# Deep sub-products of a down projection added from PSUM into running totals, with double weight tiles and a wider spread

## The chip, the cores and the metric

One core of a Trainium2 chip runs the kernel. The metric is the device time of one execution in microseconds; the time before is a median of 3 runs. TensorE (PE) multiplies, VectorE (DVE) and ScalarE (ACT) work element by element, GpSimd (POOL) and SyncE (SP) here mostly start DMAs.

## What is computed

A decoder layer on 512 tokens, model width 2048, fp32: attention in two head groups, then a gated feed-forward part with a causal convolution of width 3, then a final RMSNorm. The change lies in the feed-forward part:

```python
def conv_ffn(h, w_up, conv_w, conv_b, w_down):
    u, g = jnp.split(h @ w_up, 2, axis=-1)
    u = lax.conv_general_dilated(u, conv_w[:, None, :], ..., feature_group_count=D_FF) + conv_b
    return (jax.nn.silu(u) * g) @ w_down
...
    mod = c_act @ w_mod[l] + b_mod[l]
...
    x = x + g2 * conv_ffn(h, w_up[l], conv_w[l], conv_b[l], w_down[l])
return rms_norm(x, norm_final)
```

The hidden width is 5632: 44 tiles of 128 columns, in 11 groups of 4 (g = 0 to 10).

## The kernel before

Every fp32 product is made of three fp32r matmuls: each operand is cut into a high part (a cast on ScalarE) and a low part (a subtraction on VectorE), and high x high, low x high and high x low are summed in PSUM.

**Up slots.** A tile f of the hidden width needs two units, u and g, each of four slots; a slot loads 256 KB of w_up through SP (`raw`, 5 buffers), splits it (4 buffers of each part) and issues 12 matmuls of 128x512. So a group has 32 up slots. After unit g of a tile, `conv_gen` makes the convolution, silu and the gate.

**Down products.** The down projection of group g-1 runs among the up slots of group g. A 2x2 block scheme with seven products is used (L1066 to L1241). Four of them, `PLAIN` = 0, 2, 3, 5, run twice (for two halves of columns, c), as `Product`: 12 matmuls each. The other three, `DEEP` = 1, 4, 6, are cut once more by the same scheme into seven sub-products of 3 matmuls, class `Deep`, in four steps: sub-products (0, 1), (2, 3), (4, 5), (6). `Quads` loads the weight blocks (256 KB tiles `rq`), the `STEPS` and `STEPS2` tables say which blocks are added on VectorE before and after a split, and `cut_w` (L1082) splits a 128x512 block into `dh` and `dl`, 4 buffers each.

**Where sums go.** `total[h][dq]` are eight DRAM tiles of 512 KB. A plain product is combined on VectorE straight from PSUM (`plus`, L1162) and added to totals by accumulating DMAs on POOL's queue (`add_up`, L1116). A deep product isn't: each of its seven results is moved by ScalarE into a pair tile (L1230; the ring `two` has 3 pair tiles) and added by an accumulating DMA to a DRAM tile `part[i, j]` of its own, four DMAs a product. Only after the last group does `join_gen` (L1243) load the parts through SP, make the seven sums of each deep product on VectorE (`JOIN`, L1262), add the totals (L1270), transpose (`cT`, TensorE) and add the result, times its gate, to the residual x (`x2b`, L1280).

**The order of slots.** For groups 1 to 10, three up slots (`LEAD`), then 20 down products and 20 up slots in turn, then the other 9 up slots. In group 10 the mark `join` is set behind the 20 pairs: there the pool `pd` is closed, `pe` opens in its place, x is loaded from DRAM (`x2b`, 4 x 1 MB, SP) and `join_gen` is started, one step a slot. Then come `last_slots`: the last group's down projection in plain form, two halves of the tokens x 4 column blocks x 4 slots of 12 matmuls of 128x256. Its weights (`wd`, 16 x 256 KB, SP) are split into the space of the up operands h2h and h2l. A final norm (`finish_half`) closes each half.

**The modulation stream.** `mod_gen` (L236) makes one group of columns of the modulation from 16 pieces: a 256 KB load through SP and one VectorE multiply-add into `macc` (L207) a piece, then column sums on TensorE (`mps`, two passes of 4 matmuls), then an addition of the bias. `pace(gen, every)` calls it for one step each time TensorE has been given `every` more columns. Four groups (20 to 23) run beside groups 0 and 1, with tiles of `pd`.

A planner (the tile framework) fixes the order on each engine from priorities in program order and from what is ready by its own estimate; at run time every engine runs its queue in that order.

```python
    slots += up[:LEAD]
    products = down_products(g - 1)
    for x, y in zip(products, up[LEAD:]):
        slots += [x, y]
    if g == SG:
        marks["join"] = len(slots)
    slots += up[LEAD + len(products):]
```

Of the kernel before, what the change touches and what calls it, by code (L numbers as in the profile page):

```python
# [33 lines left out]
def hybrid_trunk(ctx, tc, xT, cT, wm, bm, nrm, wik, wiq, wi1, sinks, kvn, wuk, wuv, rel, onehot,  # L34
# [201 lines left out]
    def mod_gen(groups, load, depth, mp, get, per):  # L236
# [4 lines left out]
        for i, (g, kt) in enumerate(pieces):  # L241
# [740 lines left out]
    DH, LEAD = 4, 3  # L982
# [82 lines left out]
    class Quads:  # L1065


        BUFS = {0: 4, 1: 2, 2: 4, 3: 4}
# [4 lines left out]
        def load(self, i, c):  # L1073
            if (i, 0, c) in self.b:
# [21 lines left out]
    STEPS2 = [((), 0, ((0, 1, 0),), 0),  # L1096
              ((), 2, (), 1),
              (((1, 3, 1), (0, 3, "t")), "t", (("t", 2, 2),), 3),
              ((), 1, (), 4),
              ((), 2, (), 2),  # L1100
              ((), 0, (), 6),
              ((), 3, (), 5)]

    SIGN = [1, 1, -1, -1, 1, -1, -1]

    JOIN = ((2, 0), (1, 0), (3, 2), (6, 2), (4, 3), (6, 5), (5, 3))
    RESULT = {(0, 0): 1, (0, 1): 6, (1, 0): 4, (1, 1): 5}
    part = {(i, j): dram.tile([P, 2, T], F32, name=f"part{i}_{j}") for i in DEEP for j in range(4)}

# [6 lines left out]
    def add_up(g, to, x):  # L1116
        if g:
# [4 lines left out]
    class Product:  # L1122
# [9 lines left out]
        def split(self):  # L1132
            if self.w is None:
                self.load()
                _, before, blk, behind = STEPS[self.i]
                b, c, rows = self.quads.b, self.c, range(2)
                for p in rows:
                    for x, y, z in before:
                        dve.tensor_tensor(b[z, p, c], b[x, p, c], b[y, p, c], OP.add)  # L1139
                self.w = [cut_w(b[blk, p, c], f"{self.g}_{self.i}_{c}_{p}") for p in rows]  # L1140
                for p in rows:
                    for x, y, z in behind:
# [418 lines left out]
```

## Time and profile before

| | |
|---|---|
| time, median of 3 runs | 2205.28 us (2203.07 to 2211.99) |
| the profiled execution | 2205.46 us, its span 2203.4 us |
| busy: TensorE, VectorE, ScalarE, GpSimd | 2136.7, 1691.1, 1159.0, 249.2 us |
| chain that ended last, by engine | TensorE 80%, VectorE 7%, DMA 5%, ScalarE 4%, issue 3% |
| DMA | 438.18 MB, mean 199 GB/s |
| mean granted TensorE clock | 0.989 |
| accumulates to part / to total | 120 / 80 DMAs |
| down weights rq | 200 DMAs of 256 KB |

Busy times are shares of one execution with stages of different kinds: attention to about 600 us, its output projection to 774 us, the feed-forward part from there. Matmuls are pipelined and their ends modelled, so a row's duration overlaps the next; the distance between starts is what one costs.

### The profile page before, as it was taken

How to read it: one execution, taken by the hardware profiler on the slowest of the kernel's cores; microseconds unless marked ns; L12 is line 12 of the kernel's file. 1: busy time of each engine (PE TensorE's matmuls, PEld its weight loads, DVE VectorE, ACT ScalarE, POOL GpSimd, SP SyncE). 2: the span in 40 equal slices, each digit the busy share in tenths (PEclk: the TensorE clock that was granted, in tenths of full speed). 3: DMA queues.
4: the chain of work that ended last, by engine and by line, in shares of the span. 5: the costliest groups of instructions: out<-in, count | busy, mean ns of one | idle time of the engine just before them, and what ended most of it. 6: DMA issues, size and time to landing. Idle time of an engine off the chain costs nothing.

```text
span 2203.4 us, 30851 instructions
## 1 busy us (share of the span) xinstructions
PE 2136.7 (97%) x10286; PEld 1734.3 (79%) x10286; DVE 1691.1 (77%) x3193; ACT 1159.0 (53%) x2290; POOL 249.2 (11%) x368
## 2 busy tenths in 40 slices
PE   7999998999999999999999999999999999999976
PEld 4777776777778877888888888888888888888866
DVE  3887899777677678987868686877877686877677
ACT  5334977777622263464646555464645555554622
POOL 0000000111133100010201011110201020110200
PEclk9999999999999999999999999999999999999999
DMA  9782221676598648776949696786949596886982
GB/s 390 267 296 80 63 72 56 205 216 209 184 338 273 223 147 279 253 249 150 241 127 228 162 207 191 172 231 153 247 123 242 152 211 176 183 222 147 211 279 100
DMA packets 180800, 438.18 MB, mean 199 GB/s; under 512 B 20703, under 2 KB 27887, under 8 KB 174496
## 3 DMA queue, kind: packets, MB, share of 16 engines
q1 hardware_dynamic: 136256, 286.80, 38.9%
q0 software_dynamic: 43520, 147.84, 30.8%
q8 instruction: 80, 1.31, 0.2%
q10 hardware_dynamic: 864, 1.57, 0.2%
q14 instruction: 80, 0.66, 0.1%
HBM read 328.92 MB, written 107.22 MB: 198 GB/s over the span
## 4 chain that ended last, share of the span: by engine, by line
PE 80%; DVE 7%; DMA 5%; ACT 4%; issue 3%; POOL 0%; SPq 0%; DVEq 0%; POOLq 0%; ACTq 0%
PE p L53 10%; PE qip L53 4%; DMA mraw<-in_wm_dram 3%; PE ckv L53 1%; PE mrow L53 1%; PE p_3s L53 1%; PE p_2s L53 1%; PE p_6s L53 1%; PE p_5s L53 1%; PE p_4s L53 1%; PE p_1s L53 1%; PE p_0s L53 1%; PE o L53 1%; DVE macc L207 1%; DVE wk L668 1%
## 5 line engine op out<-in xcount | busy, mean ns | idle before, releaser
L207 DVE SCALAR_TENSOR_TENSOR macc<-mraw,cact,macc 128x512 f32<-128x512 f32 x240 | 179.7, 749 | 16.6 <-DMA mraw<-in_wm_dram 13.9
L193 ACT CAST dh<-rq 128x512 fp32r<-128x512 f32 x160 | 99.2, 622 | 103.7 <-DVE rq L1139 54.0
L194 DVE TENSOR_TENSOR dl<-rq,dh 128x512 fp32r<-128x512 f32 x160 | 109.2, 688 | 27.4 <-ACT dh L193 25.9
L53 PE MATMUL p<-dl,ah 128*128 128x512 f32 x320 | 124.5, 389 | 0.0
L53 PE MATMUL p<-dh,ah 128*128 128x512 f32 x320 | 124.5, 389 | 0.0
L53 PE MATMUL p<-dh,al 128*128 128x512 f32 x320 | 124.5, 389 | 0.0
L53 PEld LDWEIGHTS p<-dl,ah 128*128 128x128 f32 x320 | 60.1, 188 | 12.5
L53 PEld LDWEIGHTS p<-dh,ah 128*128 128x128 f32 x320 | 60.1, 188 | 12.5
L53 PEld LDWEIGHTS p<-dh,al 128*128 128x128 f32 x320 | 60.1, 188 | 12.5
L1384 POOL DMA_DIRECT2D mraw<-in_wm_dram x48 | 25.5, 532 | 351.1 <-DVE macc L207 232.1
L1432 POOL DMA_DIRECT2D mraw<-in_wm_dram x96 | 51.6, 538 | 116.7 <-DVE macc L207 83.8
L1118 POOL DMA_DIRECT2D total<-e x18 | 15.3, 852 | 366.8 <-ACT e L1170 366.8
L193 ACT CAST bh<-op 128x256 fp32r<-128x256 f32 (+1 forms) x120 | 42.3, 378 | 24.2 <-DVE op L1059 23.1
L1139 DVE TENSOR_TENSOR rq<-rq,rq 128x512 f32<-128x512 f32 x80 | 53.2, 686 | 1.6 <-DMA rq<-in_wdn_dram 1.3
L1143 DVE TENSOR_TENSOR rq<-rq,rq 128x512 f32<-128x512 f32 x80 | 53.4, 688 | 0.9
L523 DVE TENSOR_TENSOR qi<-qi,qip 128x512 f32<-128x512 f32 x56 | 38.3, 685 | 14.4 <-PE qip L53 13.6
L194 DVE TENSOR_TENSOR bl<-op,bh 128x256 fp32r<-128x256 f32 (+1 forms) x120 | 44.7, 388 | 3.4 <-ACT bh L193 0.6
L785 ACT ACTIVATE sb<-sb,nmb 128x512 f32<-128x512 f32 (+2 forms) x64 | 35.3, 553 | 14.7 <-DVE nmb L783 14.7
L422 DVE SCALAR_TENSOR_TENSOR macc<-mraw,cact,macc 128x512 f32<-128x512 f32 x54 | 40.4, 748 | 0.4
L1118 POOL DMA_DIRECT2D total<-u x18 | 15.3, 850 | 192.4 <-DVE u L1162 192.4
L53 PEld LDWEIGHTS mps<-ones,macc 128*128 128x128 f32 x192 | 25.4, 198 | 13.0 <-issue 9.3
L783 DVE CUSTOM_DVE_ANT_0 sb<-scb,tbb 128x512 f32<-128x512 f32 (+2 forms) x64 | 28.5, 487 | 8.6 <-PE scb L53 8.5
(4578 smaller groups left out, 7291.4 us busy)
## 6 DMA issues: line engine op xcount, KB each, us to landing
rq<-in_wdn_dram SPq DMA_DIRECT2D x200, 256.0 KB
mraw<-in_wm_dram SPq DMA_DIRECT2D x32, 1024.0 KB
mraw<-in_wm_dram POOLq DMA_DIRECT2D x48, 512.0 KB, 6.6
mraw<-in_wm_dram POOLq DMA_DIRECT2D x96, 256.0 KB, 5.3
mraw<-in_wm_dram SPq DMA_DIRECT2D x64, 256.0 KB
part<-e_0s POOLq DMA_DIRECT2D x30, 512.0 KB, 8.0
part<-e_2s POOLq DMA_DIRECT2D x30, 512.0 KB, 8.1
part<-e_4s POOLq DMA_DIRECT2D x30, 512.0 KB, 7.8
```

The costliest lines, as they stand in the source:

```text
L53: return self.to.matmul(out, w, x, **kw)
L193: act.copy(hi_t, full)
L194: dve.tensor_tensor(lo_t, full, hi_t.bitcast(F32), OP.subtract)
L207: tc.keep_in_program_order(dve.scalar_tensor_tensor(acc, t, cact[:, kt:kt + 1], acc, OP.mult, OP.add))
L422: dve.scalar_tensor_tensor(acc, fetched[j, q][:, kt % 4], cact[:, kt:kt + 1], acc, OP.mult, OP.add)
L523: dve.tensor_tensor(qi[i], qi[i], ps, OP.add)
L783: dve.tensor_tensor_reduce(s[:, o:o + n], where[b], bias, 1.0, self.nsk, OP.add, OP.min, accum_out=nm[:, b:b + 1])
L785: act.activation(s[:, o:o + n], s[:, o:o + n], AF.Exp, bias=nm[:, b:b + 1], scale=-1.0, accum_out=den[:, b:b + 1])
L1118: pool.dma_start(to, x, accum_op=OP.add)
L1139: dve.tensor_tensor(b[z, p, c], b[x, p, c], b[y, p, c], OP.add)
L1143: dve.tensor_tensor(b[z, p, c], b[x, p, c], b[y, p, c], OP.add)
L1432: pool.dma_start(t, wm[g, kt // 4][:, kt % 4])
```

## The change

Each deep product is combined on VectorE from PSUM, as the plain ones are: step 0 moves one result by ScalarE, the other six (one of them used twice) are added or subtracted by seven VectorE operations into two pair tiles r0 and r1, which are added to the same totals by two accumulating DMAs (`more=True`: also for group 0). The steps become (0, 1), (2), (3, 6), (5, 4). `part`, `JOIN` and `RESULT` go, and so does the summing in `join_gen`; it loads the totals by POOL into four tiles `ct` and transposes from these.

Weight blocks of two rows are one tile of 128x2x512: half as many loads, block sums, casts and subtractions, each twice as wide; half as many buffers.

The slots are spread wider: two up slots behind each of a deep product's first three steps (in group 10, one behind its second), one behind the others. So the products end with the up slots; in group 10 three up slots remain behind the join, in place of nine.

The modulation stream beside groups 0 and 1 gets one empty step ahead of each column sum (`gap`), and its steps come each 3100 columns in place of 3300.

```diff
-    def mod_gen(groups, load, depth, mp, get, per):
+    def mod_gen(groups, load, depth, mp, get, per, gap=0):
...
             if kt == KT - 1:
+                for _ in range(gap):
+                    yield
                 ps = get(f"mps{g}")
...
-        BUFS = {0: 4, 1: 2, 2: 4, 3: 4}
+        BUFS = {0: 2, 1: 1, 2: 2, 3: 2}
...
-            for p in range(2):
-                t = env["pd"].tile([P, 512], F32, tag=f"rq{tag}", bufs=self.BUFS[tag], name=f"rq{self.g}_{i}_{c}_{p}")
-                sp.dma_start(t, wdn[self.g, c + 2 * (at % 2)][:, 2 * (at // 2) + p])
-                self.b[i, p, c] = t
+            t = env["pd"].tile([P, 2, 512], F32, tag=f"rq{tag}", bufs=self.BUFS[tag], name=f"rq{self.g}_{i}_{c}")
+            sp.dma_start(t, wdn[self.g, c + 2 * (at % 2)][:, 2 * (at // 2):2 * (at // 2) + 2])
+            self.b[i, c] = t
     def cut_w(x, n):
-        hi_t = env["pd"].tile([P, 512], F32R, tag="dh", bufs=DH, name=f"dh{n}")
-        lo_t = env["pd"].tile([P, 512], F32R, tag="dl", bufs=DH, name=f"dl{n}")
-        split_to(hi_t, lo_t, x)
-        return hi_t, lo_t
+        hi_t = env["pd"].tile([P, 2, 512], F32R, tag="dh", bufs=2, name=f"dh{n}")
+        lo_t = env["pd"].tile([P, 2, 512], F32R, tag="dl", bufs=2, name=f"dl{n}")
+        k = x.shape[1]
+        split_to(hi_t[:, :k], lo_t[:, :k], x)
+        return [(hi_t[:, i], lo_t[:, i]) for i in range(k)]
...
+    STEPS2 = [((0, 1), (), 0, ((0, 1, 0),)),
+              ((2,), ((1, 3, 1), (0, 3, "t")), "t", (("t", 2, 2),)),
+              ((3, 6), (), 1, ()),
+              ((5, 4), (), 0, ())]
+    OPERAND = [0, 1, 3, 4, 2, 6, 5]
...
-    def add_up(g, to, x):
-        if g:
+    def add_up(g, to, x, more=False):
+        if g or more:
             pool.dma_start(to, x, accum_op=OP.add)
...
         def out(self):
-            g, i, j0, n = self.g, self.i, self.subs[0], len(self.subs)
-            t = pair_tile(f"e{g}_{i}_{j0}s")
-            for k, (j, ps) in enumerate(zip(self.subs, self.ps)):
-                act.mul(t[:, k], ps, float(SIGN[i] * SIGN[j]))
-            add_up(g, part[i, j0 // 2][:, :n], t[:, :n])
+
+            i, box = self.i, self.box
+            n = f"{self.g}_{i}s"
+            h, dq = {1: (0, 0), 4: (1, 0), 6: (0, 2)}[i]
+
+            def plus(to, x, j):
+                dve.tensor_tensor(to, x, self.ps[j], OP.add if SIGN[i] * SIGN[j] > 0 else OP.subtract)
+
+            if self.step == 0:
+                box["r1"] = pair_tile(f"r1{n}")
+                act.mul(box["r1"][:, 0], self.ps[0], float(SIGN[i] * SIGN[0]))
+                box["r0"] = pair_tile(f"r0{n}")
+                plus(box["r0"][:, 0], box["r1"][:, 0], 1)
+                return
+            r0, r1 = box["r0"], box["r1"]
+            if self.step == 1:
+                plus(r1[:, 0], r1[:, 0], 2)
+            elif self.step == 2:
+                plus(r0[:, 1], r1[:, 0], 3)
+                plus(r1[:, 0], r1[:, 0], 6)
+            else:
+                plus(r1[:, 1], r0[:, 1], 5)
+                plus(r1[:, 0], r1[:, 0], 5)
+                add_up(self.g, total[h][dq + 1], r1, True)
+                plus(r0[:, 1], r0[:, 1], 4)
+                add_up(self.g, total[h][dq], r0, True)
...
-        yield from deep(1, 0, 0)
-        yield from deep(4, 1, 0)
...
+        for dq in range(4):
+            ct = []
+            for h in range(2):
+                t = env["pe"].tile([P, 2, T], F32, tag="ct", bufs=4, name=f"ct{dq}_{h}")
+                pool.dma_start(t, total[h][dq])
+                ct += [t[:, 0], t[:, 1]]
             for i in range(4):
                 ps = p_ps(f"cT{dq}_{i}", (P, 4, P))
                 for tb in range(NB):
-                    pe.transpose(ps[:, tb], ready[tb, dq][:, P * i:P * i + P], ident)
+                    pe.transpose(ps[:, tb], ct[tb][:, P * i:P * i + P], ident)
...
-        products = down_products(g - 1)
-        for x, y in zip(products, up[LEAD:]):
-            slots += [x, y]
+        at = LEAD
+        for i, x in enumerate(down_products(g - 1)):
+            n = 1 if i < 8 or i % 4 == 3 else 2
+            if g == SG and i % 4 == 1:
+                n = 1
+            slots += [x] + up[at:at + n]
+            at += n
         if g == SG:
             marks["join"] = len(slots)
-        slots += up[LEAD + len(products):]
+        slots += up[at:]
...
-    pace(mod_gen(range(20, 24), pd_mod, 4, p2, o_bank, 1), 3300)
+    pace(mod_gen(range(20, 24), pd_mod, 4, p2, o_bank, 1, 1), 3100)
```

## Rows read from the trace of the kernel before

**Rows 1.** The page, busy time, share of the span and instructions.

```profile
PE 2136.7 (97%) x10286; PEld 1734.3 (79%) x10286; DVE 1691.1 (77%) x3193; ACT 1159.0 (53%) x2290; POOL 249.2 (11%) x368
```

**Rows 2.** The chain in order of time: start us, us, what.

```profile
1003.36 8.16 PE u8ps L53 x36
...
1988.00 8.16 PE u40ps L53 x36
```

**Rows 3.** TensorE's timeline in group 0: start us, us, engine, line, operation.

```profile
865.67 1.75 PE L53 MATMUL mps<-ones,macc 128*128 128x1 f32 x8 [4.17 <-DVE macc L207]
867.29 0.77 PE L53 MATMUL g3ps<-h2h,g3r_1h 128*128 128x512 f32 x1
...
873.04 0.40 PE L53 MATMUL g3ps<-h2h,g3r_2l 128*128 128x512 f32 x1
```

**Rows 4.** The chain's last stretch.

```profile
2159.51 1.10 PE d_1ps L53 x7
...
2187.11 1.45 PE d_3ps L53 x12
```

**Rows 5.** TensorE's timeline, transposes of the join.

```profile
2127.16 1.31 PE L57 MATMUL cT<-identr,res 128*128 128x128 f32 x8 [0.41 <-DVE x2b L1280]
```

**Rows 6.** Windows at the end: stretch us, busy by engine, granted clock, DMA, GB/s.

```profile
2090.00:2100.00 10.00, 10.00 (x45) 8.28 (x45) 2.72 (x5) 1.87 (x3) 0.00 (x0) 1.00 1.02 394
2105.00:2110.00 5.00, 1.75 (x7) 0.77 (x5) 4.34 (x8) 1.24 (x2) 0.00 (x0) 0.82 0.62 187
2110.00:2115.00 5.00, 4.49 (x12) 3.11 (x11) 3.78 (x7) 0.62 (x1) 0.00 (x0) 0.50 1.00 336
2105.00:2160.00 55.00, 40.07 (x247) 32.39 (x246) 46.76 (x82) 14.07 (x27) 0.00 (x0) 0.94 0.65 216
2140.00:2145.00 5.00, 2.75 (x21) 2.34 (x20) 5.00 (x9) 1.21 (x2) 0.00 (x0) 1.00 0.57 163
```

**Rows 7.** Waits from 2083.7 to 2170: total us, times, longest us.

```profile
ACT h2h L193 <- DMA wd<-in_wdn_dram: 23.5, 9, 3.8
...
SPq L1249 <- DVE sub L1262: 6.2, 2, 4.1
...
SPq L1469 <- PE p_6s L53: 3.3, 1, 3.3
```

**Rows 8.** Groups by line and shape: count, busy us, mean ns.

```profile
L194 DVE TENSOR_TENSOR dl<-rq,dh 128x512 fp32r<-128x512 f32 x160 | 109.2, 688 | 27.4 <-ACT dh L193 25.9
...
L1162 DVE TENSOR_TENSOR v<-e,p 128x512 f32<-128x512 f32 x40 | 27.2, 680 | 0.6
...
L1230 ACT ACTIVATE e_0s<-p_0s 128x512 f32<-128x512 f32 x30 | 17.9, 598 | 6.2 <-PE p_0s L53 5.5 <-PE p_1s L53 0.6
...
L194 DVE TENSOR_TENSOR al<-cu,ah 128x256 fp32r<-128x256 f32 x40 | 16.7, 420 | 0.0
```

**Rows 9.** Window over one steady group.

```profile
1345.40:1468.50 123.10, 123.10 (x544) 101.93 (x544) 92.86 (x164) 66.45 (x122) 17.06 (x20) 1.00 0.77 191
```

**Rows 10.** Timelines of VectorE and TensorE: a weight split and its first use.

```profile
1449.79 0.68 DVE L154 TENSOR_TENSOR g22r_0l<-g22r,g22r_0h 128x512 fp32r<-128x512 f32 x1
...
1461.29 0.39 PE L53 MATMUL g22ps<-h2h,g22r_0l 128*128 128x512 f32 x1
```

**Rows 11.** Groups by line and shape from 2083.7 to 2160: one of the join's.

```profile
L1262 DVE TENSOR_TENSOR res<-res,sub 128x512 f32<-128x512 f32 x12 | 8.1, 686 | 3.7 <-DMA sub<-part 3.7
```

**Rows 12.** SP's timeline at the join: start us, us, DMA issues.

```profile
2083.68 2.84 SPq L1469 DMA_DIRECT2D x2b<-x2d  x4
...
2092.05 3.46 SPq L1249 DMA_DIRECT2D sub<-part  x2
...
2101.07 0.32 SPq L1249 DMA_DIRECT2D sum<-total  x1
```

**Rows 13.** DMA issues: count, KB each, median us to landing.

```profile
total<-u POOLq DMA_DIRECT2D x20, 512.0 KB, 5.4
...
total<-v POOLq DMA_DIRECT2D x20, 512.0 KB, 9.1
```

More of the change, by code (lines that the diff above doesn't have):

```diff
@@ L981, in hybrid_trunk @@
     acts, ugate = {}, {}
-    DH, LEAD = 4, 3
+    LEAD = 3
     def u_after(f):
@@ L1135, in split @@
                 _, before, blk, behind = STEPS[self.i]
[L1136 to L1142, printed above, removed]
-                        dve.tensor_tensor(b[z, p, c], b[x, p, c], b[y, p, c], OP.add)
+                b, c = self.quads.b, self.c
+                for x, y, z in before:
+                    dve.tensor_tensor(b[z, c], b[x, c], b[y, c], OP.add)
+                self.w = cut_w(b[blk, c], f"{self.g}_{self.i}_{c}")
+                for x, y, z in behind:
+                    dve.tensor_tensor(b[z, c], b[x, c], b[y, c], OP.add)
         def mm(self, w):
@@ L1186, in hybrid_trunk, with __init__ @@
     class Deep:
-        def __init__(self, g, i, subs, quads):
-            self.g, self.i, self.subs, self.quads, self.w, self.after = g, i, subs, quads, None, self.out
+        def __init__(self, g, i, step, quads, box):
+            self.g, self.i, self.step, self.quads, self.box, self.w, self.after = g, i, step, quads, box, None, self.out
         def load(self):
@@ L1238, in down_products @@
         for i in DEEP:
-            res += [Deep(g, i, j, quads) for j in ((0, 1), (2, 3), (4, 5), (6,))]
+            box = {}
+            res += [Deep(g, i, step, quads, box) for step in range(4)]
         return res
@@ L1245, in join_gen @@
         dve.tensor_scalar(neg, mod[:, 21:23], -1.0, None, OP.mult)
-        ready = {}
-        def load(t, x):
-            sp.dma_start(t, x)
-            return t
-        def deep(i, h, dq):
-            r = {j: load(env["pe"].tile([P, T], F32, tag="res", bufs=8, name=f"res{i}_{j}"), part[i, j // 2][:, j % 2])
-                 for j in (1, 4, 5, 6)}
-            t = pair_tile(f"sub{i}_0")
-            r[0] = load(t[:, 0], part[i, 0][:, 0])
-            t = load(pair_tile(f"sub{i}_2"), part[i, 1])
-            r[2], r[3] = t[:, 0], t[:, 1]
-            yield
-            for n, (x, y) in enumerate(JOIN):
-                dve.tensor_tensor(r[x], r[x], r[y], OP.add)
-                if n == 3:
-                    yield
-            for c in range(2):
-                t = load(pair_tile(f"sum{h}_{dq + c}"), total[h][dq + c])
-                yield
-                for b in range(2):
-                    x = r[RESULT[b, c]]
-                    dve.tensor_tensor(x, x, t[:, b], OP.add)
-                    ready[2 * h + b, dq + c] = x
-        def turned(dq):
+        for dq in range(4):
[4 more added lines that the diff above has]
+                ct += [t[:, 0], t[:, 1]]
             for i in range(4):
@@ L1282, in turned @@
                     yield
-        yield from deep(1, 0, 0)
-        yield from deep(4, 1, 0)
-        for dq in range(2):
-            yield from turned(dq)
-        yield from deep(6, 0, 2)
-        for dq in range(2, 4):
-            t = load(pair_tile(f"sum1_{dq}"), total[1][dq])
-            for b in range(2):
-                ready[2 + b, dq] = t[:, b]
-            yield from turned(dq)
     def last_slots(dq, half):
```

47 lines of the change are left out of this document (17 added, 30 removed).

## The prediction

> **What bounds the kernel now.** I read the page first: TensorE is busy for 97% of the span [rows 1]. A busy share says little where matmuls are pipelined, so the second look is at the chain in order of time, where the feed-forward groups repeat. Between the starts of two groups eight groups apart lie 984.64 us, 123.08 us a group [rows 2]. A group has 32 up slots of 12 matmuls, 8 plain products of 12 and 3 times 7 sub-products of 3: 384 + 96 + 63 = 543. An up slot takes 2.72 us (three of them in 8.16 us [rows 2]), 0.2267 us a matmul, and 543 of these are 123.08 us. So these groups have no gap at all, and nothing the change does to VectorE, ScalarE or the DMAs there can make them shorter; it can only keep them or open gaps. What can be won lies where TensorE does wait, and two such places touch the changed lines.
>
> The first is in group 0, within up unit g3: the column sums of the modulation (mps) wait 4.17 us for macc, and the 13 matmuls behind them take 5.75 us, 867.29 to 873.04, where 2.95 are due [rows 3]. The hole is worth about 7.0 us.
>
> The second is the end. Group 10 starts at 1988.00 and would end its up slots at 1988.00 + 123.08 = 2111.1. Then come, at TensorE's own rate, 12 slots of the last group's first half (12 x 1.44 = 17.3, from 12 matmuls in 1.45 us [rows 4]) and 64 transposes (8 in 1.31 us [rows 5]: 10.5), so the last unbroken stretch could begin at 2138.9. It begins at 2159.5 [rows 4]: a hole of 20.6 us. From there it is 29.05 us of matmuls to 2188.6 and 14.8 us of closing norm and output to 2203.4; neither is changed. In the hole VectorE is busy 46.76 of 55 us and TensorE 40.07; the granted clock falls to 0.82 and 0.50 of full, which is the 1.2 GHz level, behind TensorE's pause at 2105 [rows 6]. ScalarE waits 23.5 us for the last down weights, and SP holds these up: its queue stands 6.2 us before part and total loads whose tiles VectorE has not freed [rows 7].
>
> **The change, part by part.** *Sub-products in PSUM.* Per deep product seven ScalarE moves (598 ns each) become one; seven VectorE operations with one PSUM operand come in. The same form exists: 680 ns, against 688 for two SBUF operands [rows 8], so PSUM costs nothing extra. Per group that is 18 x 0.60 = 10.8 us less on ScalarE and 21 x 0.68 = 14.3 us more on VectorE. *Two rows as one.* A 1024-wide operation isn't in the trace; from 420 ns at 256 and 688 at 512 the slope is 268 ns per 256, so it should take 1.22 us, 0.15 us less than two (bounds: nothing, as the second of two already overlaps the first, and 0.15). Per group 17 pairs of splits and 8 of block sums: 25 x 0.15 = 3.8 us off VectorE. VectorE's 92.86 us of a group [rows 9] become 103.4 of 123.1. I cost this at nothing: TensorE covers it, and weight splits stand well ahead, e.g. one ended at 1450.47 and was read at 1461.29 [rows 10]. With 4 up and 2 deep slots in place of 4 and 4 among the ring's four buffers that lead shrinks by 2.7 to some 8 us. Two double buffers for split weights hold as much as four single ones; the second-next product lies over 8 us behind the one that frees them, and cast plus subtract take 2.3.
>
> *DMAs.* Per deep product four accumulates (1.75 MB) become two (1.05 MB), and the down weights load in half as many, double transfers. DMAs fill 0.77 of a group [rows 9] and bound nothing there: no time, either way. POOL's accumulates now wait for VectorE; behind them in its queue stand only later accumulates and, at the end, the loads of totals.
>
> *gap=1 and 3100.* Steps between the last macc and its mps go from one of 3300 columns to two of 3100: 1.4 us of cover becomes 2.6. The stream as a whole is no slower (18 x 3100 against 17 x 3300 columns a group). The wait is 4.17 us, so 1.2 us more cover alone leaves 3; but macc pieces also run 6% faster. Bounds: all 7.0 us back, or none. I take half, 3.5, since the cover won is a third of the wait and shorter waits spare the slow clock too.
>
> *The spread.* In the last group 6 more up slots now lie ahead of the join: 16.3 us. *The join.* It loses 33 VectorE operations (21 sums of parts, 12 with totals; 0.69 us each, 0.60 where they follow one another: 19.8 us) [rows 11] and 5.5 MB of part loads; totals (4.2 MB) are now loaded by POOL, into tiles that feed the transposes directly. SP keeps the four x2b loads and the last down weights, so these no longer queue behind parts. VectorE's 46.8 us in the hole become 27. Against that, x2b is released only by the last deep matmul: SP waits 3.3 us for p_6s [rows 7]. Its four loads were issued at 2083.7 and landed between 2092.0 and some 2101: 8.4 to 17.4 us [rows 7, 12]. That was 27 us ahead of the up slots' end; it will be 2100.0, 11 us ahead.
>
> So, the new end: x2b (4.2 MB), the last two accumulates (1.05) and the first four total tiles (2.1) want the DMAs at once, 7.3 MB. At the 394 GB/s of a full stretch [rows 6] this is 18.6 us, to 2118.6. TensorE has from 2111.1 two slots whose weights were loaded before (2.9 us) and 32 transposes (5.2), about to 2119.2 if the tiles arrive in a good order. I take 4 us of idling, for the down weights behind x2b, and 3 for the slow clock after it (the price in group 0): a hole of 7 in place of 20.6, **13 us won** (rounded down). Bounds: 0 to 20.6.
>
> The Trainium skill (DMA: Bandwidth & Descriptors, section Issuing engines are not separate DMA queues) says that transfers begun by SP, ACT or GpSimd run on the same 16 DMA engines and interleave. That speaks against moving the totals to POOL as a gain; were the queues separate, x2b alone would take 10.6 us and the hole would close, giving 2182. The trace has SP's queue nearly alone at a share of 1.02 [rows 6], which fits; no run here shows both at once yet.
>
> The sum stands against the profiled execution, 2205.46 us, which is 2.06 us over its span and 0.2 us over the median of the runs: 2205.46 - 13 - 3.5 = **2189**.
>
> **The rivals.** *The hole only moves* (2203). The late x2b, the totals and the down weights share one pool of DMA engines. If the down weights come last, TensorE idles from 2114.0 to about 2121, runs 3 us at the slow clock, and the second four total tiles, which wait for the first transposes and then for their landing (5.4 to 9.1 us for accumulates of that size [rows 13]), cost another 8: a hole of 18, and 2205.5 - 2.6 = 2203 with no gain in group 0. For it: the full DMA share [rows 6]; against it: 5.5 MB less to move and VectorE no longer full (5.00 of 5 us at 2140 [rows 6]).
>
> *Both holes close* (2178): 2205.5 - 20.6 - 7.0. It needs the tiles in just the order in which they are wanted.
>
> *Totals wait on totals* (2219, slower). The ring has three pair tiles; each deep product holds two until its accumulates land. The next deep product's r0 needs the tile of the last one's r1. With T the end of a product's last matmul, r1 is done at about T+1.1 and landed at T+6.5 to T+10.2 (5.4 to 9.1 us [rows 13]); r0 is due at T+4.4, one up slot and two sub-products later. VectorE would stand 2 to 6 us in 20 places, with the splits of the next up weights queued behind. This decides once the stand exceeds the lead of some 8 us; 1.5 us over it at 20 places is 30 us, 2205.5 + 30 - 16.5. Against it: the lead, and that the order can put other work first.
>
> *It does nothing* (2205): the holes come from something else, such as the order in which x2b is updated.
>
> **How the numbers follow.** Forecast 2189, on its own 2181 to 2197 (tail gain 7 to 17, group 0 gain 1.5 to 7): 0.50. The hole moves: 0.27. Both close: 0.12. Slower: 0.08. Nothing: 0.03. About 0.5% (11 us) is what a measurement of this kernel can tell from no change. Faster by more, below 2194.4: 0.41 of the forecast, 0.12, and 0.05 of the second case: 0.58. Slower by more: 0.08. The rest, 0.34, is within. Leaving out the slower case and the outer half of the case in which both close gives 2179 to 2206.
>
> **What would show it.** The groups from 2 to 9 still 123.08 us apart; any other figure speaks for the slower rival, and then VectorE's waits before r0 name a DMA on total. VectorE near 103 us of a group. The wait of mps for macc below 4.17 us and matmuls 0.227 us apart behind it. x2b loads issued at the end of the last deep matmul, 11 us before the up slots' end, and the final unbroken stretch beginning 13 us (with group 0's part 16 to 17) earlier. I am wrong if that stretch begins within 5 us of where it does now, or if x2b is released earlier than by the last deep product.

## The result, and the profile after

The changed kernel takes 2195.54 us (median of 6 runs, 2192.77 to 2197.56) beside 2204.97 us of the kernel before in the same runs: a ratio of 0.995, 95% interval 0.9935 to 0.9966. The forecast was 2189, on its own 2181 to 2197, with a range of 2179 to 2206 over all cases. The profiled execution has 2194.85 us and a span of 2192.8, 10.6 us shorter than the span before.

The same views as in [rows 1, 2, 9]: the page's busy times, the chain at the starts of groups 2 and 10 (start us, us, what), and the window over one steady group (busy us and count of PE, PEld, DVE, ACT, POOL; granted clock, DMA share, GB/s):

```profile
PE 2130.0 (97%) x10286; PEld 1733.6 (79%) x10286; DVE 1769.3 (81%) x3120; ACT 1048.6 (48%) x1940; POOL 206.1 (9%) x316
...
1000.33 8.16 PE u8ps L53 x36
...
1984.97 8.16 PE u40ps L53 x36
...
1369.57:1492.65 123.08, 123.08 (x545) 101.95 (x544) 102.72 (x160) 55.52 (x88) 11.98 (x15) 1.00 0.72 171
```

Eight groups still take 984.64 us. VectorE's share of a group rose by 9.9 us, ScalarE's fell by 10.9, and neither shows in the time. So the 10.6 us lie elsewhere, and four stretches add up to them:

| stretch | before | after | difference |
|---|---|---|---|
| to the first xn row (code not touched) | 773.93 | 776.08 | +2.15 |
| groups 0 and 1 | 229.43 | 224.25 | -5.18 |
| groups 2 to 9 | 984.64 | 984.64 | 0 |
| group 10 to the end of the last matmul | 200.55 | 192.62 | -7.93 |
| closing norm and output | 14.85 | 15.2 | +0.35 |

The fourth row is the tail. As in the prediction, a stretch without any gap there would be 150.9 us from the start of group 10 (123.08 + 17.3 + 10.5) and 29.05 us of last matmuls, 179.95 together. What is over it I call the hole: 20.6 us before, **12.7 us after** (192.62 - 179.95); 7 were forecast. It is a scale for comparing kernels, not the idle time: eight transposes at full clock take 1.03 us, not the 1.31 of [rows 5], so a kernel without idling would stand at -2.3.

Where it lies is read from the queues. First SP's and GpSimd's timelines (start us, us, DMA issues, in brackets the wait ahead of them), then TensorE's, then the windows:

```profile
2085.96 11.36 SPq L147 DMA_DIRECT2D wd<-in_wdn_dram  x5
2097.38 2.07 SPq L1452 DMA_DIRECT2D x2b<-x2d  x4
...
2078.66 0.99 POOL L1262 DMA_DIRECT2D ct<-total  x1
2098.46 1.72 POOL L1113 DMA_DIRECT2D total<-r_6s  x2 [18.80 <-DVE r_6s L1223]
2099.86 1.95 POOL L1262 DMA_DIRECT2D ct<-total  x3
```

```profile
2105.21 0.39 PE L53 MATMUL g43ps<-h2l,g43r_2h 128*128 128x512 f32 x1
2118.26 1.12 PE L57 MATMUL cT<-identr,ct 128*128 128x128 f32 x4 [12.66 <-DMA ct<-total]
2119.03 0.78 PE L53 MATMUL g43ps<-h2h,g43r_2l 128*128 128x512 f32 x1
```

```profile
2105.00:2110.00 5.00, 0.60 (x3) 0.17 (x1) 0.00 (x0) 0.62 (x1) 0.00 (x0) 0.86 1.05 315
2110.00:2115.00 5.00, 0.00 (x0) 0.00 (x0) 0.00 (x0) 0.00 (x0) 0.00 (x0) 0.50 1.02 342
2115.00:2120.00 5.00, 1.74 (x7) 1.56 (x8) 1.01 (x2) 0.00 (x0) 0.00 (x0) 0.50 1.02 415
2120.00:2125.00 5.00, 5.00 (x25) 4.35 (x24) 2.14 (x4) 0.00 (x0) 1.05 (x2) 0.78 1.02 367
```

The first total tile was issued at 2078.66. The second stood in GpSimd's queue behind the last product's accumulates, which waited 18.8 us for VectorE; it was issued at about 2100, right beside x2b, and landed at 2118.26. A transpose that reads it stood in the middle of g43, so 13 ready matmuls of g43 and all later slots stood behind it for 12.66 us, with every engine idle and the DMAs full; the clock went to 0.50 of full, the 1.2 GHz level, after TensorE's pause. VectorE, which was busy for 46.76 of 55 us in the hole before [rows 6], is idle in it now.

### The profile page after: what moved, and what is told of

Read it like the earlier page. It is cut to its first block, busy times and chain, and to the rows that moved or that the text cites. A ratio compares the mean times of both kernels' runs of the same rounds, so it can differ in the third digit from the quotient of the medians.

```text
span 2192.8 us, 29799 instructions
## 1 busy us (share of the span) xinstructions
PE 2130.0 (97%) x10286; PEld 1733.6 (79%) x10286; DVE 1769.3 (81%) x3120; ACT 1048.6 (48%) x1940; POOL 206.1 (9%) x316
## 4 chain that ended last, share of the span: by engine, by line
PE 83%; DVE 5%; DMA 4%; ACT 4%; issue 3%; POOL 0%; SPq 0%; DVEq 0%; POOLq 0%; ACTq 0%
PE p L53 10%; PE qip L53 4%; DMA mraw<-in_wm_dram 2%; PE o L53 1%; PE ckv L53 1%; PE mrow L53 1%; PE p_6s L53 1%; PE p_3s L53 1%; PE p_2s L53 1%; PE p_1s L53 1%; PE p_0s L53 1%; PE p_4s L53 1%; PE p_5s L53 1%; DMA ct<-total 1%; PE mps L53 1%
## 5 line engine op out<-in xcount | busy, mean ns | idle before, releaser
L193 ACT CAST dh<-rq 128x1024 fp32r<-128x1024 f32 x80 | 84.0, 1052 | 75.0 <-PE p L53 63.1
L194 DVE TENSOR_TENSOR dl<-rq,dh 128x1024 fp32r<-128x1024 f32 x80 | 97.7, 1223 | 23.8 <-ACT dh L193 22.9
L193 ACT CAST ah<-cu 128x256 fp32r<-128x256 f32 (+1 forms) x60 | 28.8, 479 | 52.9 <-PE p L53 20.0
L193 ACT CAST dh_0s<-rq 128x1024 fp32r<-128x1024 f32 x30 | 31.6, 1055 | 38.9 <-PE p L53 21.2
L525 DVE TENSOR_TENSOR qi<-qi,qip 128x512 f32<-128x512 f32 x56 | 38.3, 684 | 14.4 <-PE qip L53 13.7
L1136 DVE TENSOR_TENSOR rq<-rq,rq 128x1024 f32<-128x1024 f32 x40 | 48.9, 1221 | 0.9
L1133 DVE TENSOR_TENSOR rq<-rq,rq 128x1024 f32<-128x1024 f32 x40 | 48.8, 1219 | 0.6 <-DMA rq<-in_wdn_dram 0.3
L194 DVE TENSOR_TENSOR bl<-op,bh 128x128 fp32r<-128x128 f32 (+1 forms) x120 | 44.4, 384 | 1.5
L1155 DVE TENSOR_TENSOR u<-v,p 128x512 f32<-128x512 f32 x40 | 27.4, 686 | 16.4 <-PE p L53 16.4
L194 DVE TENSOR_TENSOR dl_0s<-rq,dh_0s 128x1024 fp32r<-128x1024 f32 x30 | 36.7, 1224 | 3.7 <-ACT dh_0s L193 3.6
```

The costliest lines, as they stand in the source:

```text
L193: act.copy(hi_t, full)
L194: dve.tensor_tensor(lo_t, full, hi_t.bitcast(F32), OP.subtract)
L525: dve.tensor_tensor(qi[i], qi[i], ps, OP.add)
L1133: dve.tensor_tensor(b[z, c], b[x, c], b[y, c], OP.add)
L1136: dve.tensor_tensor(b[z, c], b[x, c], b[y, c], OP.add)
L1155: dve.tensor_tensor(to[:, b], x[:, b], self.ps[b], OP.add if sign > 0 else OP.subtract)
```

## Experiments

All are edits of the changed kernel. Ratios are to the kernel before, with the 95% interval; "tail" is group 10's start to the end of the last matmul, and the hole is the tail less 179.95. Ratios are what to compare, as each was taken beside its own runs of the kernel before, whose medians are 2204.97 to 2207.47 us. Of them only those of the kernel with the blocks apart (faster) and of the narrow spread everywhere (slower) lie clear of the change's interval. A hole comes from one profile each. For the kernels that keep the new modulation stream and the spread of groups 1 to 9, the median less the hole is 2182.0 to 2185.6 us, so holes less than some 4 us apart are not told apart by the times; there the waits in the traces have to tell.

| kernel | median us | ratio | tail | hole |
|---|---|---|---|---|
| the change | 2195.5 | 0.9950 (0.9935 to 0.9966) | 192.6 | 12.7 |
| totals first on SP | 2194.5 | 0.9943 (0.9928 to 0.9958) | 189.9 | 10.0 |
| totals on ScalarE's queue | 2193.5 | 0.9936 (0.9920 to 0.9953) | 188.6 | 8.6 |
| transposes later | 2191.5 | 0.9929 (0.9913 to 0.9945) | 189.5 | 9.5 |
| old modulation | 2199.4 | 0.9966 (0.9952 to 0.9979) | 193.6 | 13.7 |
| narrow last group | 2198.8 | 0.9966 (0.9956 to 0.9975) | 194.4 | 14.4 |
| narrow, transposes later | 2195.0 | 0.9954 (0.9937 to 0.9972) | 191.8 | 11.9 |
| fewer totals | 2194.6 | 0.9952 (0.9934 to 0.9970) | 191.6 | 11.7 |
| narrow everywhere | 2209.3 | 1.0014 (1.0005 to 1.0024) | 195.1 | 15.2 |
| in order of need | 2191.4 | 0.9928 (0.9911 to 0.9944) | 186.8 | 6.8 |
| need, transposes later | 2195.5 | 0.9948 (0.9933 to 0.9963) | 191.0 | 11.1 |
| own queue, transposes later | 2194.7 | 0.9941 (0.9926 to 0.9956) | 189.1 | 9.1 |
| blocks apart | 2187.5 | 0.9913 (0.9897 to 0.9928) | 183.3 | 3.4 |

**Three theories for the hole.** A (queue): the tile was late because of what stood ahead of it in GpSimd's queue. B (volume): x2b, accumulates and totals fill the DMAs together. C (order): the transposes stand ahead of matmuls that need no tile.

*Totals first on SP.* Four `ct` loads are issued on SP ahead of x2b; `ct_load(dq, eng)` issues the two tile loads of a column block on the queue of engine `eng`.

```diff
...
+    for dq in range(2):
+        early[dq] = ct_load(dq, sp)
     for i in range(4):
         sp.dma_start(env["x2"][i], x2d[i])
```

> The loads of the first four total tiles leave GpSimd's queue and stand in SP's, just ahead of the four x2b loads, whose first is issued at 2097.38 us in the changed kernel. Theory A (queue): the tiles were late only because GpSimd's queue stood 18.8 us before the last accumulates; the start moves from 2099.86 to about 2097.4, and with the same 18.4 us of transfer they would land at 2115.8, so TensorE's wait shrinks from 12.7 to some 10 us and the time by 2.5 us, to 2193. Theory B (volume): the start matters little, what fills the 18.4 us are 4.2 MB of x2b in front of and beside the tiles; with the tiles first (2.1 MB at the 394 GB/s of a full stretch, 5.3 us, and the accumulates beside them) they land by 2103 to 2107, TensorE waits under 3 us, and the time falls by 9 to 12 us, to 2183 to 2186. Theory C (order: the transposes stand ahead of 13 matmuls and of slots that need no tile): nothing is reordered here, so it goes with whatever the landing does; it adds no number of its own.

The tiles came early, as B says: no wait for them over 3.3 us. But the hole shrank by 2.7 us only, and the time, 2194.5, is near A's 2193 for another reason than A's. The time went to x2b, which now came second: VectorE stood 9.7 us before its first update, for x2b, until 2115.89, and TensorE's transposes then waited up to 3.4 us for PSUM banks that those updates free. Each theory had looked at one wait; two loads are needed for one block.

*Totals on ScalarE's queue.* `ct_load(dq, act)` for all four blocks.

> As the kernel with the totals first on SP, but all eight tile loads are issued by ScalarE, the first four right after the activation that reads u43 at 2096.2 us, so at about 2097, side by side with SP's x2b loads at 2097.4. Theory A (queue): out of GpSimd's queue, which stood behind the accumulates; the landing moves by the 3 us of earlier start, time about 2192. Theory B (volume): x2b and the tiles start together and share the DMAs, 4.2 + 2.1 + 1.05 MB at 394 GB/s, all to about 2115; the tiles would land between 2108 and 2115 and TensorE would still wait 3 to 10 us: time 2186 to 2192. If it comes out as the kernel with the totals first (2183 to 2186), sharing is not even and the queue that a load stands in is what matters.

*Fewer totals.* Only the first pair of tiles is loaded, by GpSimd as in the change.

```diff
+        ct = []
         for dq in range(4):
-            ct = []
-            for h in range(2):
+            for h in range(0 if dq else 2):
...
```

> The changed kernel in which only the first pair of total tiles is loaded and all 64 transposes read it; the other six tiles (3.1 MB) are left out, so the result is another one. The order of TensorE and the place of every other load are those of the changed kernel. Theory A (GpSimd's queue): the second tile of the first pair is issued at 2099.9 as before; with 7.9 us of landing, the median of the loads of totals, or more it is late by 2 us and more. Theory B (volume): ahead of or beside that tile 4.2 MB of x2b and 1.05 MB of accumulates remain of 7.3 MB, so it lands 13 to 16 us after issue, at 2113 to 2116, and the wait of 12.7 us shrinks to 7 to 10 us, and since no later tile is waited for, the time falls by 4 to 8 us, to 2187 to 2191. If the wait stays at 12 us or more, the tile's time is not set by its companions but by x2b alone or by the accumulate ahead of it in its own queue.

These two belong together. ScalarE's issues, the first transposes and VectorE's first update of the one; GpSimd's issue and TensorE's wait of the other:

```profile
2098.58 0.33 ACTq L1260 DMA_DIRECT2D ct<-total  x1
2098.94 1.43 ACTq L1260 DMA_DIRECT2D ct<-total  x3
2105.18 1.03 PE L57 MATMUL cT<-identr,ct 128*128 128x128 f32 x8
2114.05 1.41 DVE L1276 SCALAR_TENSOR_TENSOR x2b<-cT,mod,x2b 128x512 f32<-128x512 f32 x2 [11.12 <-DMA x2b<-x2d]
```

```profile
2103.33 1.72 POOL L1113 DMA_DIRECT2D total<-r_6s  x2 [18.80 <-DVE r_6s L1223]
2104.74 0.87 POOL L1262 DMA_DIRECT2D ct<-total  x1
...
2122.98 1.12 PE L57 MATMUL cT<-identr,ct 128*128 128x128 f32 x4 [12.51 <-DMA ct<-total]
```

In ScalarE's queue both tiles of block 0 were read, without a wait, 6.6 us after the first issue. In GpSimd's queue, behind two accumulates, a single tile took 18.2 us, with six tile loads left out. So B in its plain form falls (it asked for 13 to 16 us and a time of 2187 to 2191).

The pair alone doesn't show A, for on ScalarE's queue the tiles were issued 1.5 us ahead of x2b and on GpSimd's 2.5 us behind it. What the queues moved does show it (packets, MB, share; GpSimd's queue, q0, from 2103 to 2118 and from 2118 to 2123 with fewer totals; then ScalarE's, q10, and SP's, q1, from 2098 to 2105 with the totals on ScalarE's queue):

```profile
q0 software_dynamic: 273, 1.04, 35.3%
q0 software_dynamic: 159, 0.53, 26.7%
```

```profile
q10 hardware_dynamic: 408, 1.53, 66.6%
q1 hardware_dynamic: 218, 0.41, 20.4%
```

Up to 2118, some 13 us after the tile's issue, GpSimd's queue moved what the two accumulates hold (2 x 512 KB), and only then one tile. A stands: the tile waited for what stood ahead of it in its queue. The issuing engine is not what made it 18 us: with the totals first on SP, GpSimd issued four later tiles with no accumulate left ahead, at a DMA share of 1.0, and these landed in 7.9 to 11.7 us. Volume has a part in it, through the accumulates, which took 13.0 us beside x2b. On ScalarE's queue the tiles also had a head start, as the second pair of rows shows: x2b had hardly begun to move when they were read.

But out of GpSimd's queue the wait only changed its place: x2b came later, and VectorE stood 11.1 us before it with the splits for the last group's slots behind. The time, 2193.5, lies above what A and B gave for it.

*Transposes later.* `start(join_gen(), 5)`.

> The changed kernel with its join begun five slots later: the first transposes stand behind all matmuls of g43 and behind the first slots of the last group instead of in the middle of g43. No load is moved in its queue. Theory C (order): TensorE keeps 13 matmuls of g43 (2.95 us) and two to four slots of 12 matmuls (1.45 us each) to do while the tiles land; of the 12.7 us of waiting 6 to 8.7 are filled, and the clock falls less: time 2186 to 2189. Theories A and B (the landing alone): the tiles still land at about 2118, and what then follows (64 transposes, 32 updates of x2b on VectorE at about 0.7 us) is merely pushed later: VectorE, idle from 2105 to 2118 before, gets the same 32 updates after 2118 and sets the end: time 2193 to 2197, and the wait reappears in the last group's slots as matmuls waiting for VectorE.

TensorE's first wait for a tile fell from 12.7 to 6.0 us and the hole from 12.7 to 9.5, about half the least that C asked, and the time lies between the two expectations; the rest came back behind: GpSimd issued the last tiles only at 2135.59, when transposes had freed their buffers. C holds in part.

*Narrow last group*, and the same with the transposes later: all counts of up slots between the deep products of group 10 are 1, so nine up slots lie behind the join.

```diff
-            if g == SG and i % 4 == 1:
+            if g == SG:
                 n = 1
```

> The changed kernel without the wider spread in the last group alone: the deep products there follow one up slot apart, so nine up slots (24.5 us) instead of three to four (11 us) lie behind the join; groups 1 to 9 keep the spread. Three arrangements of the loads left holes of 8.6 to 10.1 us behind the up slots' end where the changed kernel has 12.7. Theory B (volume against cover): x2b and the totals, released by the last deep matmul, fill the DMAs for some 27 us (share 1.00 or more from 2100 to 2125); with 16.3 us more of matmuls above that rush it ends near the up slots' end, the hole shrinks to 0 to 4 us, the time to 2183 to 2188. Rival (VectorE): the last group's deep products, 16 instead of 22 us each, crowd VectorE's sums and splits, and TensorE waits for split weights inside the group: the hole is shorter, but the group's up slots last longer than 123.08 + 3 us; time 2192 to 2196. Rival (order): the transposes stand in the middle of u43 and wait there for tiles just the same, 8 to 12 us, with the rest of the up slots behind them: 2193 to 2196.

> The narrow spread of the last group, with the join begun six slots later, so that the first transposes stand two thirds through g43, 17 us behind the last deep matmul. Theory B with order: the tiles wanted first have landed by then (18 to 21 us after their issue at most), the hole is 0 to 3 us, the time 2182 to 2186, below the kernel with the narrow spread alone by as much as that one still waits for tiles at its first transposes. If order matters nothing once there is cover: equal to the kernel with the narrow spread alone within 2 us. Rival (VectorE): 32 updates of x2b come later and share VectorE with the last slots' rows; the hole moves into the last slots, time 2186 to 2192.

More cover did not help. The first wait for a tile is TensorE's row below, from the kernel with the narrow spread alone; the second row is ScalarE's in the one with later transposes:

```profile
2105.34 1.11 PE L57 MATMUL cT<-identr,ct 128*128 128x128 f32 x4 [13.93 <-DMA ct<-total]
```

```profile
2108.49 0.62 ACT L153 CAST g43r_3h<-g43r 128x512 fp32r<-128x512 f32 x1 [12.24 <-DMA g43r<-in_wup_dram]
```

In the first the transposes simply stood earlier, in u43, before the same late tile: the rival on order. In the second they are out of the way, and the next thing late is a weight of g43, loaded by SP behind x2b: a rush that starts 13 us earlier catches up slots whose weights aren't loaded yet. Neither expectation named that. The time 2198.8 lies above all that were given for the first, and 2195.0 between the rival's 2192 and a time equal to the first's.

*Narrow everywhere.* `n = 1` in all groups.

> The changed kernel with up slots and down products alternating one by one in all groups, as in the kernel before, and nine up slots behind the last product of each group. It tells what the spread is worth in the groups 1 to 9. Theory (TensorE bounds them, VectorE has 20 us of 123 to spare): the groups stay at 123.08 us and the time is that of the kernel with the narrow spread in the last group alone, within 2 us. Rival (totals wait on totals, VectorE crowded): in 16 instead of 22 us per deep product VectorE has seven PSUM operations, four 1024-wide splits and sums and the splits of four instead of six up slots; the r0 of the next product waits for the landing of r1 of the one before, and TensorE gaps of 1 to 4 us per deep product appear, 27 of them: 125 to 131 us a group, 2210 to 2260.

It is slower than the kernel before. Groups 2 to 9 take 989.84 us in place of 984.64, and TensorE's weight loads show why (waits from 1005 to 1995: total us, times, longest us):

```profile
PEld p_3s L53 <- DVE dl_2s L194: 5.9, 8, 1.3
```

Not r0 waiting for totals, as the rival had it, but the low part of a deep product's weights, late by up to 1.3 us once in each group. The size is far below the rival's 1 to 4 us at 27 places. In groups 0 and 1 the same wait (2.4 us) and one for an up weight (1.2 us) appear as well, and its last group has a hole of 15.2 us. The theory of unchanged groups failed: the change needs the wider spread in the steady groups. For the last group alone that isn't shown, since the interval of the narrow last group (0.9956 to 0.9975) overlaps the change's.

*Old modulation.* `mod_gen(..., o_bank, 1), 3300)`.

> The changed kernel with the modulation stream put back as it was: no step left out between the last macc and its column sums, one piece every 3300 columns. Of the 9.95 us between the kernel before and after, groups 0 and 1 hold 5.2 us by the two traces (229.43 us from the first xn row to the start of u8, then 224.25). If these lines own that gain, groups 0 and 1 take about 229.4 us again, mps waits 4 us for macc, and the time is 2199 to 2201. If the gain came from somewhere else in those groups (the wider spread or the 1024-wide loads reach group 1 too), they stay at 224 to 226 and the time is 2194 to 2197. Rival on the other side: the stream shifts VectorE's work later in the groups and costs nothing: 2195.

Time 2199.4: 3.8 us over the change. In the traces the stretch from the first xn row to the first u8 matmul is 229.3 us before and 227.1 here with the old stream; with the new one it is 223.9 to 228.0 in eleven profiles, 225.9 in the mean (taken from the first matmul's own row, 0.16 us under the table above; the kernel with the narrow spread everywhere left out). The longest wait of mps for macc there runs from 1.3 to 4.5 us over the same eleven, against 4.2 before and 2.9 here. So of the expectation the time came out and its two signs didn't: 229.4 us and a wait of 4 us were to return. In that stretch the one profile lies among the eleven, 1.2 us over their mean, and the interval of the ratio, 0.9952 to 0.9979, overlaps the change's. That the new stream gains anything is therefore not shown; by these numbers it is 0 to 4 us. What makes the wait short in one profile and long in the next stays open.

**Theory D.** A block's update needs its tiles and its quarter of x2b; what counts is that both, and the weights between, land in the order in which TensorE's queue wants them.

*In order of need.* On SP: tiles and x2b of block 0, of 1, of 2, of 3, then the down weights; 6 tile buffers in place of 4.

```diff
...
+        early[dq] = ct_load(dq, sp)
+        sp.dma_start(env["x2"][dq], x2d[dq])
...
```

> The changed kernel with the loads of the tail in one queue, SP's, by need: the two total tiles and the x2b quarter of column block 0, then those of block 1, 2 and 3 (six instead of four buffers for total tiles, so that a load does not wait for a transpose); the last down weights behind them. The transposes stand in TensorE's order where they were. So far: a tile alone in GpSimd's queue behind two accumulates still took some 18 us (three of four tile loads gone, wait 12.5 us), while tiles in a queue of their own, issued beside x2b, were read 6.6 us after issue, and then VectorE stood 11.1 us before x2b. Theory D (what stands ahead in the queue decides, and the first quarter of x2b is wanted as early as the first tiles): block 0 needs 2.1 MB, 5.3 us at 394 GB/s, so both are there at about 2104 to 2107, block 1 by 2112, block 2 by 2117, block 3 by 2123; TensorE waits 1 to 3 us before each block instead of 12.7 once, VectorE under 5 us for x2b; hole 3 to 7 us, time 2185 to 2190. Rival (volume): every block is needed before the matmuls behind it in the order, the rush of some 25 us stays, and the hole is that of the other arrangements, 8.6 to 10.1 us: 2191 to 2194. Rival (down weights): they now come last, at about 2125, and ScalarE's split of them holds the slots: 2194 to 2198.

> The same order of loads in SP's queue, and the join begun four slots later: the transposes of block 0 stand behind two slots of the last group, and those of the other blocks after further slots that need no tile. Theory D with order: while blocks 0 and 1 land TensorE has the rest of g43 and the four slots of block 0 (5.8 us), VectorE isn't held by x2b with splits behind it: hole 1 to 5 us, time 2183 to 2188, the lowest of all arrangements. Rival (down weights): the slots of block 1 need weights whose loads stand behind all of x2b and the totals, 8.4 MB at 394 GB/s, 21 us, so at about 2120; TensorE has work until about 2117 and then idles 3 to 8 us for them: 2187 to 2192.

> The total tiles on ScalarE's queue as in the run before on that queue (first four at about 2098.6), x2b and the down weights on SP, and the join begun four slots later. That run left a hole of 8.6 us, of which TensorE spent 7 us waiting for banks and cuts behind VectorE's wait of 11.1 us for x2b, and 2 us for tiles. Theory D: with the transposes behind four slots, VectorE does the cuts for those slots while x2b lands (about 2115); hole 3 to 6 us, time 2185 to 2189. Rival (volume): the work only swaps its place, 8 to 10 us of hole remain: 2191 to 2194.

In order of need the hole is 6.8 us, within D's 3 to 7, although its waits were spread differently: 4.9 us of VectorE for the first quarter of x2b is its longest. The time, 2191.4, is over D's 2190 and within the 2191 to 2194 of the rival on volume, whose hole of 8.6 to 10.1 us it doesn't have. Started later, the same loads left 11.1 us: the wait of the rival on down weights, though the time, 2195.5, is above its 2187 to 2192, with TensorE standing 3.2 us for a cast of wd (the last down weights) and ScalarE up to 8.2 us for the weights, and blocks 2 and 3 still behind the accumulates (SP's third pair of tiles was issued at 2116.01, once total<-r_6s had landed). The tiles on ScalarE with later transposes gave 9.1 us: the hole of the rival on volume, 8 to 10. VectorE's next update stood behind a split of wd, whose weight ScalarE awaited for 13.0 us, and TensorE waited 9.0 us behind VectorE. Both expectations for D failed there, and the waits name the same reason: down weights were not counted among the loads that are needed in order.

*Blocks apart.* The order of need with the weights in it: blocks 0 and 1, four down weights, block 2, four, block 3; the transposes of blocks 2 and 3 follow by some slots.

```diff
+            if dq > 1:
+                for _ in range(2 if dq == 2 else 1):
+                    yield
+                sp.dma_start(env["x2"][dq], x2d[dq])
+                early[dq] = ct_load(dq, sp)
+                yield
...
```

> The order of need in SP's queue carried on: totals and x2b of blocks 0 and 1 first, then four down weights (the slots of block 1 need three of them), then x2b and totals of block 2, four more down weights, and block 3; the transposes of blocks 0 and 1 stand where they were, those of blocks 2 and 3 two to four slots later. In the run with everything in order of need, TensorE's idle time between 2100 and 2140 was some 7 us, in pieces of 0.2 to 2.0 us: 3.4 us for tiles, the rest behind VectorE's updates of x2b, 7.4 us of which waited for x2b. Theory D with cover: blocks 0 and 1 still cost some 4 us (their loads fill the DMAs to about 2112 to 2117), blocks 2 and 3 land while TensorE has the slots of blocks 0 and 1 (11.6 us) to do: hole 4 to 6 us, time 2187 to 2191. Rival (rush): x2b, totals and weights need the DMAs for the same 25 us in any order, and TensorE's work that needs none of it is 11 us of up slots and five slots of 1.45 us: about 7 us of hole stay whatever the order, time 2189 to 2193. Rival (late blocks): blocks 2 and 3 come too late and the slots of blocks 2 and 3 wait behind VectorE: hole 9 to 14 us, time 2193 to 2198.

The hole is 3.4 us, the time 2187.5, ratio 0.9913 (0.9897 to 0.9928), which lies clear of the changed kernel's interval. SP's timeline and four windows of it:

```profile
2099.92 0.85 SPq L1260 DMA_DIRECT2D ct<-total  x2
2100.82 0.42 SPq L1465 DMA_DIRECT2D x2b<-x2d  x1
2101.34 1.64 SPq L1260 DMA_DIRECT2D ct<-total  x2
2103.07 0.50 SPq L1465 DMA_DIRECT2D x2b<-x2d  x1
2103.69 3.84 SPq L147 DMA_DIRECT2D wd<-in_wdn_dram  x4
...
2112.18 0.33 SPq L1272 DMA_DIRECT2D x2b<-x2d  x1
...
2125.92 1.02 SPq L1260 DMA_DIRECT2D ct<-total  x2
```

```profile
2105.00:2110.00 5.00, 3.32 (x19) 2.65 (x19) 2.38 (x4) 0.63 (x1) 0.00 (x0) 1.00 1.04 311
...
2115.00:2120.00 5.00, 3.49 (x19) 3.28 (x20) 1.74 (x3) 0.62 (x1) 0.00 (x0) 0.75 1.02 416
2120.00:2125.00 5.00, 5.00 (x41) 5.00 (x41) 4.25 (x8) 2.48 (x4) 0.00 (x0) 0.91 1.03 411
...
2130.00:2135.00 5.00, 5.00 (x45) 5.00 (x44) 4.61 (x10) 1.86 (x5) 0.00 (x0) 1.00 1.01 401
```

The DMAs are full up to 2135, longer than in the changed kernel, and TensorE is busy without a gap from 2120 to 2160. So the rival that the rush itself costs some 7 us in any order falls, and with it B: the bytes are the same. What differs from the change is the order of the loads, their queue, and the place of two blocks' transposes, all at once; beside the kernel in order of need, which has the same queue, the hole is 3.4 us shorter, but the two ratios' intervals overlap.

## Why the prediction came out as it did

**Right.** TensorE bounds the steady groups, and nothing done to VectorE, ScalarE and the DMAs there shows: 123.08 us a group, VectorE 102.72 us where 103.4 was worked out. The 1024-wide operation takes 1.22 us, as from the slope of [rows 8] (groups by line and shape from 1000 to 1990: count, busy us, mean ns):

```profile
L194 DVE TENSOR_TENSOR dl<-rq,dh 128x1024 fp32r<-128x1024 f32 x65 | 79.5, 1223 | 20.4 <-ACT dh L193 19.5
```

x2b is issued at the end of the last deep matmul (2097.38; that matmul ends at 2097.2), 10.7 us ahead of where the up slots could end; 11 were forecast. The first tiles were worked out to land 18.6 us after that; it was 20.9. The slower rival's wait exists and is as harmless as argued (whole span: total us, times, longest us); TensorE shows no wait in groups 2 to 9:

```profile
DVE r_4s L1223 <- DMA total<-r_1s: 7.8, 4, 2.1
...
DVE r_6s L1223 <- DMA total<-r_4s: 7.7, 5, 1.7
```

**Wrong: the size of the tail's gain,** 13 us forecast, 7.9 measured: 5.1 of the 5.9 us by which the profile misses the forecast's 16.5. The term that failed is "4 us of idling, for the down weights behind x2b". The down weights that were wanted first had been issued before x2b; what was late was a total tile. Two things made it 12.66 us in place of 4. POOL's queue: the prediction named the loads of totals among what stands behind the accumulates, and gave that no price. The queue stood 18.8 us for VectorE, and the tile, issued beside x2b and behind the accumulates, took another 18.4; with no accumulate ahead, tiles came in 6.6 us on ScalarE's queue and in 7.9 to 11.7 on GpSimd's. And TensorE's order: the prediction counted two slots of the last group and the rest of g43 as cover while the tiles come; in the queue they stood behind the transposes. The condition "if the tiles arrive in a good order" carried the forecast, and the reason to doubt it was in the prediction's own text: one queue for accumulates and loads. The term beside it, 3 us for the slow clock, was too large: from 2118.26 to 2122.43 TensorE did 12 transposes and 4 matmuls in 4.2 us, which at full clock (1.03 us for 8 transposes, 0.227 for a matmul) are some 2.5, so it cost some 1.7 (an estimate from these rows).

The prediction's sign for the tail could not tell this. It asked where the last unbroken stretch begins, and that is 2141.41 in place of 2159.5, 18 us earlier, because nearly all of TensorE's idling now lies in one piece that ends at 2118.26. The length of the whole tail tells it. The last wait of TensorE ahead of that stretch (TensorE's timeline):

```profile
2141.41 1.09 PE L57 MATMUL cT<-identr,ct 128*128 128x128 f32 x8 [0.46 <-DVE x2b L1284]
```

**The rivals.** "The hole only moves" (2203) had the right picture, loads that compete and TensorE idle, but with the whole price; the hole was 12.7, between its 18 and the forecast's 7. "Both holes close" named its own condition, the tiles in just the order in which they are wanted; the kernel with the blocks apart comes nearest to it in the tail, 3.4 us, still 5.7 over a kernel without idling, and shows that most of the remaining loss was order and not bytes.

**The rule of the Trainium skill** (DMA: Bandwidth & Descriptors, section Issuing engines are not separate DMA queues), that transfers begun by different engines share the 16 DMA engines, was weighed against moving the totals to POOL. Where it speaks of sharing, the traces agree: with tiles on ScalarE's queue the share stays at 1.02 to 1.05 from 2105 to 2120, and SP's queue moves 1.70 MB in the 14 us from the issue of x2b, in place of 3.07 in the changed kernel. Where it says that several issuing engines save only issue time, the measurement differs for a load behind accumulates: 6.6 us on ScalarE's queue and 18.2 on GpSimd's, for the same tile, of which some 13 went by before the tile's data moved.

**The modulation** was put at half of 7.0 us, between bounds of all and nothing. The pair of profiles has 5.2 us there, eleven profiles of the new stream 3.4 in the mean, and the old stream put back shows no gain clear of the noise, so that 3.5 came near is luck. The mechanism, a shorter wait for macc, holds in the changed kernel's profile (1.6 us for 4.17) and not in others (up to 4.5).

**The sum.** 16.5 us were forecast. The profile has 7.9 in the tail and 5.2 in groups 0 and 1, less 2.15 in code that no edit touches and 0.35 in the closing: 10.6. By the medians the gain is 9.4.

## What to carry to other kernels

When a wait is removed ahead of a burst of loads, list for each queue what stands ahead of the first load that is wanted, and for each consumer in its own order all the loads that it needs at once; price the first that comes out of order, and not the bytes. A load that is issued behind an accumulate inherits that accumulate's wait and its landing (here 18.8 and 13.2 us); and in an engine's in-order queue, work that could be cover is none if it stands behind the waiting instruction.

## What the runs showed of the hardware that was not expected

- The two accumulates of the last product took 13.2 us to land beside x2b (9.2 is their median over the whole span), and a load issued behind them on the same queue 18.2 to 18.4 us, whether one or three loads were there.
- After TensorE's wait of 12.66 us the granted clock stood at 0.50 (1.2 GHz) into the next stretch and at 0.78 in the one behind it. Short pauses did not settle it: in the kernel with all loads in order of need, with pauses of 2.0 us at most, the clock was granted in full all through the tail, while the kernel with the blocks apart, whose pauses up to 2117 are the same within 0.1 us (1.4 at most) and which has none behind, showed 0.75 and 0.91 in two stretches. What makes the difference stays open.
- The first xn row comes at 773.9 to 779.9 us over the profiles, in code that no edit touches. Two profiles are only comparable stretch by stretch below some 6 us.
